# A chunked complex recurrence as scan instructions on phase-turned inputs

## The chip, the cores and the metric

One core of one Trainium2 chip runs the kernel. The metric is the device time of one execution in microseconds, as the median of several runs. Engines are named as in the profile: PE (TensorE matmul), PEld (its weight load), DVE (VectorE), ACT (ScalarE), POOL (GpSimd), SP (SyncE, which issues most DMAs).

## The reference, cut to what matters

One decoder layer for 2048 prompt positions and 8 x 4 sample positions, `D_MODEL` 1024. The part that is touched is the S5 group: 32 channel groups of 16 channels, each driving a diagonal complex state of 64 values.

```python
dt = jnp.exp(log_dt)[:, None]
mag = jnp.exp(dt * A_re); ph = dt * A_im
ar = mag * jnp.cos(ph); ai = mag * jnp.sin(ph)
...
# s[t] = a * s[t-1] + B u[t], complex, for each group and state
acum_r, acum_i, s_r, s_i = lax.associative_scan(_complex_affine_combine, (a_r, a_i, bu_r, bu_i), axis=0)
...
y = einsum(C_re, s_r) - einsum(C_im, s_i) + D * u
```

Beside it runs a short-convolution group, `y = B * conv3(C * xin)`, whose three projections are most of the matmuls of the same stage. The final states of the prompt are outputs too. Then follow GLU, output projection, memory attention and a ConvFFN.

## The kernel before

All large products are made three times (`mm3`, L369 to L373: high x high, high x low, low x high parts of weights and activations, 416 columns each). The prompt is cut into 5 pieces of up to 52 chunks (8 positions to a chunk, 256 chunks in all). The stages follow each other: u projection and tables (to about 190 us), the **convolution stage** (about 190 to 587 us), which carries the recurrence, then memory keys and values, output projection, attention, ConvFFN.

**Order of the work.** The order is written out by hand; each engine runs its instructions in program order. In the convolution stage a loop over 2 halves x 5 pieces x 2 channel tiles calls `lin_k` with 8 steps of 9 matmuls; after each step `hook` (L1183) runs: it pumps the weight splits (`W.pump`, L94 and L98) and the activation splits (`A.pump`: L158 and L159 or L161 and L162), and takes one step of the stream `slow`, and on every second call one of `slow2`. A stage has 160 hooks. A stream is a Python generator: every `yield` gives up one step. `slow` holds `state_inputs` (L878), `scan` (L1030) and `state_outputs` (L950); `slow2` holds `load_states` (L513) and `toeplitz` (L927), which must have finished (`lags`) before `state_outputs` goes on. Between the hooks DVE also makes the convolution from PSUM (L1160, L1165, L1092, L1179).

**The recurrence.** The state tile `st` holds, on 128 partitions (2 groups x 64 states), real and imaginary parts of 16 group pairs x 264 columns: 8 sample columns, then 256 chunk inputs as 16 blocks of 16. `state_inputs` makes them with fp32 matmuls (L905, L906, a PSUM pool `aux` of two banks) that ACT copies into `st` (L908, L909). `scan` runs inside the blocks: 15 positions x 2 parts x 4 DVE instructions over all groups and blocks (L1052, L1053, L1056, L1057: 120 instructions), then the block ends one after the other on POOL (L1063 to L1068: 75 instructions). `carry` (L1071, four DVE instructions of 450 columns, L1080 to L1084) adds the carried block ends times a power table `pw`, from within `state_outputs`; `enter` copies the shifted states into `scat` (DVE and ACT L971, sample columns on POOL L972), and fp32 matmuls (L1005, L1006) make the outputs, which ACT passes through GELU (L1007). The DMA loads `load(c + 2)` (uc, gc, tcn, three buffers each) are issued by SP before the matmuls of c.

## Time and profile before

| What | Value |
|---|---|
| Median of 3 runs | 3040.74 us (3035.06 to 3041.85) |
| The profiled execution, its own time | 3032.77 us |
| Its span, first to last instruction | 3031.0 us |
| PE busy | 2894.6 us (96%) |
| DVE busy | 1466.8 us (48%) |
| ACT busy | 1118.4 us (37%) |
| POOL busy | 1143.9 us (38%) |
| Mean granted TensorE clock | 0.980 |

A busy PE is not PE at its peak: matmuls overlap, and at the lower of its two clock levels the same matmul is busy for longer. So the stage is read by the number of matmuls in a stretch and the granted clock, beside the idle time. A wait in the profile is the idle time of an engine and the instruction that ended it.

### The profile page before, as it was taken

The numbers are of one execution on the slowest core, as the hardware profiler recorded it, in microseconds if no ns is written. First come the engines' busy times: TensorE is split into PE (matmuls) and PEld (weight loads), VectorE is DVE, ScalarE is ACT, GpSimd is POOL, SyncE is SP. The second block draws the span as 40 slices with busy tenths as digits, with TensorE's granted clock in tenths as the row PEclk, the third lists the DMA queues.
The fourth block names the chain that finished last, engine by engine and source line by source line (L and its number), as shares of the span: only waits on it lengthen the run. The fifth ranks groups of instructions, "written<-read, shape, count | busy, mean of one in ns | idle before, by whom it ended". The sixth has DMA issues, their size and how long they took to land.

```text
span 3031.0 us, 42111 instructions
## 1 busy us (share of the span) xinstructions
PE 2894.6 (96%) x15728; PEld 2804.2 (93%) x15728; DVE 1466.8 (48%) x2630; ACT 1118.4 (37%) x2168; POOL 1143.9 (38%) x1360
## 2 busy tenths in 40 slices
PE   8879989989999999999999999999999999999998
PEld 7778979879999999989999999998999999989997
DVE  6742986664444344354643333436433433364443
ACT  5334224454444445342422222224223222243333
POOL 3771356453332003343533323233232232345553
PEclk9889989999999999999999999999999999999999
DMA  8563244564352123565532211124322122134331
GB/s 225 145 171 106 79 141 134 173 186 130 111 167 79 52 66 108 196 222 170 193 109 63 63 56 57 55 63 143 98 59 60 50 62 63 56 119 127 116 107 54
DMA packets 387340, 335.95 MB, mean 111 GB/s; under 512 B 81121, under 2 KB 361239, under 8 KB 387103
## 3 DMA queue, kind: packets, MB, share of 16 engines
q1 hardware_dynamic: 364079, 299.30, 33.3%
q10 hardware_dynamic: 23056, 33.96, 3.1%
q8 instruction: 124, 2.03, 0.3%
q14 instruction: 81, 0.66, 0.1%
HBM read 259.98 MB, written 75.29 MB: 111 GB/s over the span
## 4 chain that ended last, share of the span: by engine, by line
PE 57%; DVE 2%; DMA 1%; POOL 1%; issue 1%; ACT 1%; SPq 0%; ACTq 0%; DVEq 0%; POOLq 0%
PE g L371 5%; PE g L372 5%; PE g L373 5%; PE u L372 5%; PE u L371 5%; PE u L373 5%; PE d L371 5%; PE d L372 5%; PE d L373 5%; PE mm L371 3%; PE mm L372 3%; PE mm L373 3%; DMA out_dram<-orow 1%; PE aux L372 1%; DMA araw<-h 0%
## 5 line engine op out<-in xcount | busy, mean ns | idle before, releaser
L98 POOL TENSOR_TENSOR wlo<-wraw,whi 128x512 fp32r<-128x512 f32 x489 | 647.7, 1348 | 895.8 <-ACT whi L94 845.6
L371 PE MATMUL mm<-xh,whi 128*128 128x416 f32 x1600 | 587.4, 367 | 15.7 <-DVE y L1179 7.3
L373 PE MATMUL mm<-xh,wlo 128*128 128x416 f32 x1600 | 571.7, 357 | 6.9 <-POOL wlo L98 6.9
L372 PE MATMUL mm<-xl,whi 128*128 128x416 f32 x1600 | 571.4, 357 | 4.7 <-POOL xl L159 4.7
L1926 DVE TENSOR_TENSOR xac<-d,xac 128x416 f32<-128x416 f32 x440 | 258.7, 591 | 249.4 <-PE d L373 246.4
L371 PEld LDWEIGHTS mm<-xh,whi 128*128 128x128 f32 x1600 | 310.0, 194 | 26.7 <-DVE xi L1160 6.3
L94 ACT CAST whi<-wraw 128x1024 fp32r<-128x1024 f32 x256 | 267.3, 1046 | 175.3 <-PE d L372 129.2
L371 PE MATMUL d<-acth,whi 128*128 128x416 f32 x880 | 310.9, 353 | 18.0 <-DVE xac L1926 17.0
L373 PEld LDWEIGHTS mm<-xh,wlo 128*128 128x128 f32 x1600 | 309.1, 193 | 11.6 <-POOL wlo L98 9.0
L372 PEld LDWEIGHTS mm<-xl,whi 128*128 128x128 f32 x1600 | 309.7, 194 | 9.0 <-POOL xl L159 6.5
L372 PE MATMUL u<-xl,whi 128*128 128x416 f32 x880 | 310.6, 353 | 1.4 <-POOL xl L159 0.7
L371 PE MATMUL g<-xh,whi 128*128 128x416 f32 x880 | 311.3, 354 | 0.0
L372 PE MATMUL g<-xl,whi 128*128 128x416 f32 x880 | 310.8, 353 | 0.0
L371 PE MATMUL u<-xh,whi 128*128 128x416 f32 x880 | 310.4, 353 | 0.3 <-ACT xh L158 0.2
L372 PE MATMUL d<-actl,whi 128*128 128x416 f32 x880 | 309.1, 351 | 0.2 <-DVE actl L1907 0.2
L373 PE MATMUL d<-acth,wlo 128*128 128x416 f32 x880 | 308.2, 350 | 0.0
L373 PE MATMUL g<-xh,wlo 128*128 128x416 f32 x880 | 306.3, 348 | 0.0
L373 PE MATMUL u<-xh,wlo 128*128 128x416 f32 x880 | 305.9, 348 | 0.0
L1092 DVE SCALAR_TENSOR_TENSOR t<-E,par,t 128x416 f32<-128x416 f32 (+1 forms) x220 | 153.9, 700 | 265.5 <-ACT t L1894 262.8
L159 POOL TENSOR_TENSOR xl<-araw,xh 128x416 fp32r<-128x416 f32 x100 | 116.0, 1164 | 380.1 <-ACT xh L158 354.2
L371 PEld LDWEIGHTS d<-acth,whi 128*128 128x128 f32 x880 | 166.2, 189 | 26.1 <-DVE xac L1926 23.8
L1903 DVE TENSOR_TENSOR t<-t,g 128x416 f32<-128x416 f32 x110 | 64.6, 587 | 258.1 <-PE g L373 257.9
(423 smaller groups left out, 4963.4 us busy)
## 6 DMA issues: line engine op xcount, KB each, us to landing
wraw<-in_w_up_dram SPq DMA_DIRECT2D x66, 512.0 KB
wraw<-in_w_gate_dram SPq DMA_DIRECT2D x66, 512.0 KB
wraw<-in_w_down_dram SPq DMA_DIRECT2D x66, 512.0 KB
araw<-x SPq DMA_DIRECT2D x120, 208.0 KB
xres<-x SPq DMA_DIRECT2D x80, 208.0 KB
x<-xo ACTq DMA_DIRECT2D x80, 208.0 KB
x<-xT ACTq DMA_DIRECT2D x40, 208.0 KB
araw<-oo SPq DMA_DIRECT2D x40, 208.0 KB
```

What stands on the lines that cost most here:

```text
L94: self.nc.scalar.copy(out=hi, in_=r)
L98: eng.tensor_tensor(out=lo[:, s], in0=r[:, s], in1=hi[:, s], op=ALU.subtract)
L159: (eng or nc.vector).tensor_tensor(out=lo[:, 0:n], in0=src, in1=hi[:, 0:n], op=ALU.subtract)
L371: PE.matmul(ps, lhsT=wh, rhs=xh, start=start, stop=False)
L372: PE.matmul(ps, lhsT=wh, rhs=xl, start=False, stop=False)
L373: PE.matmul(ps, lhsT=wl, rhs=xh, start=False, stop=stop)
L1092: V.scalar_tensor_tensor(out=out[:, 0:n], in0=E[:, tap * w:tap * w + n], scalar=c, in1=out[:, 0:n], op0=ALU.mult, op1=ALU.add)
L1903: V.tensor_tensor(out=t, in0=t, in1=ps_[:, 0:NP], op=ALU.mult)
L1926: V.tensor_tensor(out=x, in0=ps[:, 0:NP], in1=x, op=ALU.add)
```

## The change

`scan` no longer steps through the positions. The input of position j in a block is multiplied by the unit phase exp(-i j theta) of its state (`turn`), after which the recurrence has a real factor, and one `tensor_tensor_scan` over the 256 columns runs each part (`scan_blocks`); its multiplier table `dz` holds the magnitude, with zeros where a block starts. The 16 block ends are carried in the same way, two scans over all groups. `back` adds the carries times the powers of the magnitude `rp` and makes the two products of the turn back; `enter` combines them into `scat`. `turn` and `scan_blocks` are issued from the loop of `state_inputs`, one and two group pairs behind the matmuls; one `turn` in three is on POOL. The tables `ph`, `ek`, `rp` come from `phases`, stepped by `state_inputs`; `pw` and its 24 POOL products in `tables` are gone. uc, gc and tcn have two buffers, and `load(c + 2)` comes after the matmuls of c. `state_ffn_conv` is loaded one stage later, and four tiles move to a pool that opens after the convolution stage. The diff, cut to its core:

```diff
-    stf = cp.tile([128, 352], F32, name="stf")
     stc = cp.tile([128, 64], F32, name="stc")
...
-    qs = cp.tile([128, 8, 32], F32, name="qs")
-    fbp = cp.tile([128, 2, NF], F32, name="fbp")
...
+    def load_state(pl, dst, src, parts):
+        for o, n in parts:
+            r = pl.tile([128, 128], F32, tag="sr", name="sr", bufs=2)
+            SY.dma_start(out=r[0:n, :], in_=src.rearrange("b s (f p) -> (b s f) p", p=128)[o:o + n, :])
...
-    pw = cp.tile([128, 2, 16, 16], F32, name="pw")
     a4 = cp.tile([128, 2, 16], F32, name="a4")
+    qc = cp.tile([128, 2, 16], F32, name="qc")
+    mg = cp.tile([128, 16], F32, name="mg")
...
+        G.tensor_copy(out=mg, in_=mag)
+        G.tensor_scalar(out=qc[:, 0], in0=cm, scalar1=1.0, scalar2=None, op0=ALU.add)
+        G.tensor_copy(out=qc[:, 1], in_=sn)
...
-        G.tensor_copy(out=pw[:, :, :, 0], in_=pa[:, :, 8, :])
-        for m in (1, 2, 4, 8):
-            sh = [128, 16, m]
-            cmul(pre, pw[:, 0, :, m:2 * m], pw[:, 1, :, m:2 * m], pw[:, 0, :, 0:m], pw[:, 1, :, 0:m],
-                 pw[:, 0, :, m - 1:m].to_broadcast(sh), pw[:, 1, :, m - 1:m].to_broadcast(sh), sh, f"cw{m}", G)
-            yield PAUSE
...
-        uc = py.tile([128, 2, NCH], F32, tag="uc", name="uc", bufs=3)
...
+    ph = sp_.tile([128, 2, 16, 16], F32, name="ph")
+    ek = sp_.tile([128, 2, 16, 16], F32, name="ek")
...
+    def phases():
+
+        def square(q):
+            d = sp_.tile([128, 2, 16], F32, tag="sqr", name="sqr", bufs=4)
+            cmul(sp_, d[:, 0], d[:, 1], q[:, 0], q[:, 1], q[:, 0], q[:, 1], [128, 16], "csq")
+            return d
...
+        q = qc
+        for _ in range(3):
+            q = square(q)
+        unit(q)
+        yield PAUSE
...
+        V.tensor_copy(out=ph[:, :, :, 1], in_=q)
+        for m in (2, 4, 8):
+            q = square(q)
+            double(ph, m, q)
+            yield PAUSE
+        q = square(q)
+        unit(q)
+        yield "tables"
+        for m in (1, 2, 4, 8):
+            V.tensor_tensor(out=rp[:, :, m:2 * m], in0=rp[:, :, 0:m], in1=rp[:, :, m - 1:m].to_broadcast([128, 16, m]), op=ALU.mult)
...
+        for m in (2, 4, 8):
+            q = square(q)
+            double(ek, m, q)
+            yield PAUSE
...
+    def product_tile(t):
+        return sp_.tile(SQ, F32, tag="m" + t, name="m" + t, bufs=1 if t == "c" else 2)
+
+    def blocks(c):
+        return st[:, :, c, 8:264].rearrange("p r (k j) -> p r k j", j=16)
+
+    def turn(c, eng):
+
+        x, m2 = blocks(c), product_tile("b")
+        eng.tensor_tensor(out=m2, in0=x[:, ::-1], in1=ph[:, 1, c].unsqueeze(1).unsqueeze(1).to_broadcast(SQ), op=ALU.mult)
+        eng.tensor_tensor(out=x, in0=x, in1=ph[:, 0, c].unsqueeze(1).unsqueeze(1).to_broadcast(SQ), op=ALU.mult)
+        for r, op in ((0, ALU.add), (1, ALU.subtract)):
+            eng.tensor_tensor(out=x[:, r], in0=x[:, r], in1=m2[:, r], op=op)
+
+    def scan_blocks(c):
+
+        S.copy(out=dz[:, :, 1:16], in_=rp[:, c, 0:1].unsqueeze(1).to_broadcast([128, 16, 15]))
+        for r in range(2):
+            x = st[:, r, c, 8:264]
+            V.tensor_tensor_scan(out=x, data0=dz.rearrange("p k j -> p (k j)"), data1=x, initial=0.0, op0=ALU.mult, op1=ALU.add)
...
+            gc = py.tile([128, 2, 2, 128], F32, tag="tcn", name="gc", bufs=2)[:, :, 0, :]
...
+        tb = phases()
         load(0)
         usv = us_d.rearrange("(g p) j b -> j p g b", p=16)
         for j in range(NT):
             SY.dma_start(out=us_[16 * j:16 * j + 16, 1], in_=usv[j])
         load(1)
-        for _ in range(5):
-            yield PAUSE
+        for step in tb:
+            if step == "tables":
+                break
+            yield step
         V.tensor_copy(out=us_[64:128, 0], in_=us_[0:64, 1])
-        for _ in range(6):
+        for _ in range(4):
             yield PAUSE
         for c in range(16):
...
-            if c + 2 < 16:
-                load(c + 2)
...
-            yield PAUSE
+            if c + 2 < 16:
+                load(c + 2)
+            if c > 0:
+                turn(c - 1, G if c % 3 == 1 else V)
+            if c > 1:
+                scan_blocks(c - 2)
+            yield PAUSE
+            next(tb, None)
             if c % 4 == 3:
                 yield PAUSE
+        turn(15, V)
+        scan_blocks(14)
...
+        yield PAUSE
+        scan_blocks(15)
+        for _ in tb:
+            yield PAUSE
+        for _ in range(6):
...
-            tc_ = py.tile([128, 2, 2, 128], F32, tag="tcn", name="tcn", bufs=3)
...
+        def back(c):
+
+            x, m2, t = blocks(c), product_tile("b"), product_tile("c")
+            V.tensor_tensor(out=t, in0=ek[:, :, c].unsqueeze(3).to_broadcast(SQ),
+                            in1=rp[:, c].unsqueeze(1).unsqueeze(1).to_broadcast(SQ), op=ALU.mult)
+            V.tensor_tensor(out=x, in0=x, in1=t, op=ALU.add)
+            V.tensor_tensor(out=m2, in0=x[:, ::-1], in1=ph[:, 1, c].unsqueeze(1).unsqueeze(1).to_broadcast(SQ), op=ALU.mult)
+            G.tensor_tensor(out=x, in0=x, in1=ph[:, 0, c].unsqueeze(1).unsqueeze(1).to_broadcast(SQ), op=ALU.mult)
+            parts[c] = [m.rearrange("p r k j -> p r (k j)") for m in (x, m2)]
...
-            sc = py.tile([128, 2, 264], F32, tag="scat", name="scat", bufs=2)
+            sc = py.tile([128, 2, 256], F32, tag="scat", name="scat", bufs=2)
             V.memset(sc[:, :, 0:1], 0.0)
+            m1, m2 = parts.pop(c)
             for a in range(2):
                 h = slice(a * 64, (a + 1) * 64)
                 for r in range(2):
-                    o = sc[r * 64:(r + 1) * 64, a]
-                    (S.copy if r else V.tensor_copy)(out=o[:, 1:256], in_=st[h, r, c, 8:263])
-                    G.tensor_copy(out=o[:, 256:264], in_=s0[h, r, :, c])
+                    (G if r else V).tensor_tensor(out=sc[r * 64:(r + 1) * 64, a, 1:256], in0=m1[h, r, 0:255],
+                                                  in1=m2[h, r, 0:255], op=ALU.add if r else ALU.subtract)
+            for r in range(2):
+                G.tensor_tensor(out=sfin[:, r, c:c + 1], in0=m1[:, r, 255:256], in1=m2[:, r, 255:256],
+                                op=ALU.add if r else ALU.subtract)
...
-        for r in range(2):
-            carry(0, r)
-            yield PAUSE
-        for _ in range(6):
-            yield PAUSE
+        back(0)
+        yield PAUSE
+        yield PAUSE
         enter(0)
+        back(1)
         for _ in range(3):
             yield PAUSE
         for c in range(16):
-            if c + 2 < 16:
-                load(c + 2)
-            if c < 14:
-                carry(c // 2 * 2 + 2, c % 2)
             if c + 1 < 16:
                 enter(c + 1)
+            if c + 2 < 16:
+                back(c + 2)
             yield PAUSE
             uc, tcn, oc = ld.pop(c)
             sc = ent_.pop(c)
...
-                    PE.matmul(ps[:, o], lhsT=oc[:, i, :], rhs=sc[:, i, o], start=False, stop=True)
+                    PE.matmul(ps[:, o], lhsT=oc[:, i, :], rhs=sc[:, i, :] if o.start == 0 else s0s[:, 2 * c + i, :],
+                              start=False, stop=True)
                 S.activation(out=yg[:, i, :], in_=ps[:, 0:264], func=AF.Gelu_apprx_tanh)
+            if c + 2 < 16:
+                load(c + 2)
...
-            for r in range(2):
-                t = sp_.tile([128, 16, 16], F32, tag="sc", name="sc", bufs=2)
-                V.tensor_tensor(out=t, in0=x[:, r, :, :, j - 1], in1=ab[:, r], op=ALU.mult)
-                V.tensor_tensor(out=x[:, r, :, :, j], in0=x[:, r, :, :, j], in1=t, op=ALU.add)
-                yield
-                t = sp_.tile([128, 16, 16], F32, tag="sc", name="sc", bufs=2)
-                V.tensor_tensor(out=t, in0=x[:, 1 - r, :, :, j - 1], in1=ib[:, r], op=ALU.mult)
-                V.tensor_tensor(out=x[:, r, :, :, j], in0=x[:, r, :, :, j], in1=t, op=ALU.add)
-                yield
-
...
-            prev, cur = x[:, :, :, k - 1, 15], x[:, :, :, k, 15]
-            t = sp_.tile([128, 2, 16], F32, tag="cc", name="cc", bufs=2)
-            G.tensor_tensor(out=t, in0=prev, in1=pw[:, 0:1, :, 15].to_broadcast([128, 2, 16]), op=ALU.mult)
-            u = sp_.tile([128, 2, 16], F32, tag="cc", name="cc", bufs=2)
-            G.tensor_tensor(out=u, in0=prev[:, ::-1], in1=pw[:, 1:2, :, 15].to_broadcast([128, 2, 16]), op=ALU.mult)
-            G.tensor_tensor(out=cur, in0=cur, in1=t, op=ALU.add)
-            G.tensor_tensor(out=cur[:, 0], in0=cur[:, 0], in1=u[:, 0], op=ALU.subtract)
-            G.tensor_tensor(out=cur[:, 1], in0=cur[:, 1], in1=u[:, 1], op=ALU.add)
-            yield PAUSE
...
-    def carry(g0, r):
-
-        gs = slice(g0, g0 + 2)
-        sh = [128, 2, 15, 15]
-        x = st[:, :, :, 8:264].rearrange("p r g (k j) -> p r g k j", j=16)
-        c = [x[:, i, gs, 0:15, 15:16].to_broadcast(sh) for i in range(2)]
-        pb = [pw[:, i, gs, 0:15].unsqueeze(2).to_broadcast(sh) for i in range(2)]
-        d = x[:, r, gs, 1:16, 0:15]
-        t = sp_.tile(sh, F32, tag="sc", name="sc", bufs=2)
-        V.tensor_tensor(out=t, in0=c[r], in1=pb[0], op=ALU.mult)
-        V.tensor_tensor(out=d, in0=d, in1=t, op=ALU.add)
-        t = sp_.tile(sh, F32, tag="sc", name="sc", bufs=2)
-        V.tensor_tensor(out=t, in0=c[1 - r], in1=pb[1], op=ALU.mult)
-        V.tensor_tensor(out=d, in0=d, in1=t, op=ALU.add if r else ALU.subtract)
...
+        last = st[:, :, :, 8:264].rearrange("p r g (k j) -> p r g k j", j=16)[:, :, :, :, 15]
+        m2, e = product_tile("b"), product_tile("b")
+        V.tensor_copy(out=dz[:, :, 1:16], in_=rp[:, :, 15:16].to_broadcast([128, 16, 15]))
+        V.tensor_tensor(out=e, in0=last, in1=ek[:, 0:1].to_broadcast(SQ), op=ALU.mult)
+        V.tensor_tensor(out=m2, in0=last[:, ::-1], in1=ek[:, 1:2].to_broadcast(SQ), op=ALU.mult)
+        V.tensor_tensor(out=e[:, 0], in0=e[:, 0], in1=m2[:, 0], op=ALU.add)
+        V.tensor_tensor(out=e[:, 1], in0=e[:, 1], in1=m2[:, 1], op=ALU.subtract)
+        yield
+        ev = e.rearrange("p r g k -> p r (g k)")
+        for r in range(2):
+            V.tensor_tensor_scan(out=ev[:, r], data0=dz.rearrange("p g k -> p (g k)"), data1=ev[:, r],
+                                 initial=0.0, op0=ALU.mult, op1=ALU.add)
...
+        V.tensor_tensor(out=m1[:, :, :, ks], in0=e[:, :, :, 0:15], in1=ek[:, 0:1, :, ks].to_broadcast(SC), op=ALU.mult)
+        V.tensor_tensor(out=m2[:, :, :, ks], in0=e[:, ::-1, :, 0:15], in1=ek[:, 1:2, :, ks].to_broadcast(SC), op=ALU.mult)
+        for r, op in ((0, ALU.subtract), (1, ALU.add)):
+            V.tensor_tensor(out=ek[:, r, :, ks], in0=m1[:, r, :, ks], in1=m2[:, r, :, ks], op=op)
+        V.memset(ek[:, :, :, 0:1], 0.0)
+        yield
...
-    slow2.add(load_states())
+    slow2.add(load_state(py, stc, I["state_conv"][0], [(0, 64)]))
     slow2.add(toeplitz())
```

## Rows read from the trace of the kernel before

**Rows 1.** Page, part 1: busy time, share of the span, instructions.
```profile
PE 2894.6 (96%) x15728; PEld 2804.2 (93%) x15728; DVE 1466.8 (48%) x2630; ACT 1118.4 (37%) x2168; POOL 1143.9 (38%) x1360
```

**Rows 2.** Stretches: us, busy (count) PE, PEld, DVE, ACT, POOL, PEclk, DMA share, GB/s.
```profile
216.00:281.00 65.00, 54.18 (x278) 50.47 (x279) 12.83 (x22) 34.43 (x83) 12.51 (x12) 0.91 0.49 147
305.00:445.00 140.00, 123.24 (x589) 115.91 (x588) 130.04 (x191) 36.17 (x65) 56.51 (x56) 0.90 0.39 113
445.00:487.00 42.00, 42.00 (x224) 41.55 (x224) 23.99 (x35) 15.94 (x30) 36.12 (x87) 1.00 0.38 114
487.00:587.00 100.00, 91.66 (x497) 85.99 (x495) 72.92 (x147) 40.59 (x95) 49.94 (x103) 0.95 0.52 157
```

**Rows 3.** The same stretches, only instructions on the PSUM tile mm (no POOL column).
```profile
305.00:445.00 140.00, 123.11 (x587) 115.64 (x586) 13.38 (x25) 0.00 (x0) 0.90 0.39 113
445.00:487.00 42.00, 42.00 (x224) 41.51 (x223) 4.93 (x9) 0.00 (x0) 1.00 0.38 114
487.00:587.00 100.00, 49.66 (x236) 44.28 (x234) 8.38 (x16) 0.00 (x0) 0.95 0.52 157
```

**Rows 4.** Waits of PE from 195 to 500 us: total us, times, longest.
```profile
PE aux L905 <- DMA gc<-g_d: 8.8, 3, 4.6
...
PE mm L371 <- DVE y L1179: 7.3, 5, 2.1
PE mm L371 <- DVE xi L1160: 5.2, 2, 3.3
PE mm L373 <- POOL wlo L98: 4.0, 2, 2.2
...
PE aux L1006 <- DVE scat L971: 4.6, 1, 4.6
```

**Rows 5.** Tile st: duration ns min/median/max, first and last start, forms.
```profile
L971 DVE COPY scat<-st x32: 277/289/1242, 491.0 to 583.5; 64x255 f32<-64x255 f32 x32
L1052 DVE TENSOR_TENSOR sc<-st,ar x30: 578/606/1575, 305.1 to 441.7; 128x256 f32<-128x256 f32 x30
...
L1083 DVE TENSOR_TENSOR sc<-st,pw x16: 621/624/1698, 475.5 to 573.3; 128x450 f32<-128x450 f32 x16
```

**Rows 6.** Timeline of DVE (two rows) and POOL (one): start us, us, instruction.
```profile
310.56 0.60 DVE L1056 TENSOR_TENSOR sc<-st,ai 128x256 f32<-128x256 f32 x1
311.19 1.35 DVE L1057 TENSOR_TENSOR st<-st,sc 128x256 f32<-128x256 f32 x1
...
310.54 1.51 POOL L159 TENSOR_TENSOR xl<-araw,xh 128x416 fp32r<-128x416 f32 x1 [3.16 <-ACT xh L158]
```

**Rows 7.** Groups by line, 300 to 450 us: busy us, mean ns | idle before.
```profile
L1052 DVE TENSOR_TENSOR sc<-st,ar 128x256 f32<-128x256 f32 x30 | 28.3, 943 | 0.0
...
L1053 DVE TENSOR_TENSOR st<-st,sc 128x256 f32<-128x256 f32 x30 | 23.9, 796 | 1.0
```

**Rows 8.** Lines of like shape elsewhere: ns min/median/max, first and last start, forms.
```profile
L565 DVE TENSOR_TENSOR pk<-pk,cpk x4: 691/1432/1432, 96.4 to 163.4; 128x512 f32<-128x512 f32 x4
L565 DVE TENSOR_TENSOR bb<-bb,cbb x1: 424/424/424, 87.4 to 87.4; 128x256 f32<-128x256 f32 x1
...
L1032 DVE TENSOR_SCALAR ai<-pw x1: 163/163/163, 296.6 to 296.6; 128x16 f32<-128x16 f32 x1
...
L584 POOL TENSOR_TENSOR ogt<-ctn,pat x12: 1049/1056/1495, 109.0 to 172.1; 128x512 f32<-128x512 f32 x12
...
L1666 POOL TENSOR_TENSOR skl<-ckv,skh x32: 723/864/1811, 1315.4 to 1384.7; 128x256 fp32r<-128x256 f32 x32
```

**Rows 9.** Timeline of PE, two successive half pairs of the output matmuls.
```profile
578.54 0.68 PE L1005 MATMUL aux<-uc,tcn 128*128 128x256 f32 x2
...
579.85 0.68 PE L1005 MATMUL aux<-uc,tcn 128*128 128x256 f32 x2
```

**Rows 10.** Groups of POOL by line, 487 to 587 us.
```profile
L972 POOL COPY scat<-s 64x8 f32<-64x8 f32 x64 | 25.8, 403 | 2.5
```

**Rows 11.** Waits of the SP queue, 195 to 610 us.
```profile
SPq L875 <- PE aux L906: 6.9, 6, 3.0
```

More of the change, by code (lines that the diff above doesn't have):

```diff
@@ L276, in tile_hymba_step @@
     V.memset(halc, 0.0)
-    stf = cp.tile([128, 352], F32, name="stf")
     stc = cp.tile([128, 64], F32, name="stc")
-    qs = cp.tile([128, 8, 32], F32, name="qs")
-    fbp = cp.tile([128, 2, NF], F32, name="fbp")
-    fbs = cp.tile([128, 8, 2, NF], F32, name="fbs")
     cbp = cp.tile([128, 2, 4], F32, name="cbp")
@@ L511, in load_params @@
         yield PAUSE
-    def load_states():
-        fl = I["state_ffn_conv"][0].rearrange("b s (f p) -> (b s f) p", p=128)
-        cl = I["state_conv"][0].rearrange("b s (f p) -> (b s f) p", p=128)
-        for dst, src, o, n in ((stf, fl, 0, 128), (stf, fl, 128, 128), (stf, fl, 256, 96), (stc, cl, 0, 64)):
-            r = py.tile([128, 128], F32, tag="sr", name="sr", bufs=2)
-            SY.dma_start(out=r[0:n, :], in_=src[o:o + n, :])
+    def load_state(pl, dst, src, parts):
+        for o, n in parts:
+            r = pl.tile([128, 128], F32, tag="sr", name="sr", bufs=2)
+            SY.dma_start(out=r[0:n, :], in_=src.rearrange("b s (f p) -> (b s f) p", p=128)[o:o + n, :])
             for _ in range(6 if o else 8):
@@ L870, in load_u @@
     def load_u(c):
-        uc = py.tile([128, 2, NCH], F32, tag="uc", name="uc", bufs=3)
+        uc = py.tile([128, 2, NCH], F32, tag="uc", name="uc", bufs=2)
         for i in range(2):
@@ L883, in load @@
             uc = load_u(c)
-            gc = py.tile([128, 2, 2, 128], F32, tag="tcn", name="gc", bufs=3)[:, :, 0, :]
+            gc = py.tile([128, 2, 2, 128], F32, tag="tcn", name="gc", bufs=2)[:, :, 0, :]
             SY.dma_start(out=gc, in_=g_d[:, g2, :])
@@ L917, in state_inputs @@
             rs_.append(r)
-        for _ in range(7):
+        yield PAUSE
[3 more added lines that the diff above has]
+        for _ in range(6):
             yield PAUSE
@@ L923, in state_inputs @@
             V.tensor_copy(out=s0[:, i].rearrange("p b g -> p (b g)"), in_=ps[:, 0:128])
+            sv = s0s.rearrange("p (g a) b -> p a b g", a=2)
+            for a in range(2):
+                G.tensor_copy(out=sv[i * 64:(i + 1) * 64, a], in_=s0[a * 64:(a + 1) * 64, i])
     lags = [0]
@@ L958, in load @@
             uc = load_u(c)
-            tc_ = py.tile([128, 2, 2, 128], F32, tag="tcn", name="tcn", bufs=3)
+            tc_ = py.tile([128, 2, 2, 128], F32, tag="tcn", name="tcn", bufs=2)
             SY.dma_start(out=tc_, in_=to_d[:, g2])
             ld[c] = (uc, tc_[:, :, 0, :], tc_[:, :, 1, :])
+        parts = {}
+        def back(c):
[6 more added lines that the diff above has]
+            parts[c] = [m.rearrange("p r k j -> p r (k j)") for m in (x, m2)]
         def enter(c):
-            sc = py.tile([128, 2, 264], F32, tag="scat", name="scat", bufs=2)
+            sc = py.tile([128, 2, 256], F32, tag="scat", name="scat", bufs=2)
             V.memset(sc[:, :, 0:1], 0.0)
+            m1, m2 = parts.pop(c)
             for a in range(2):
@@ L1013, in state_outputs @@
             store(out=ysd[j], in_=ysm[j * 16:(j + 1) * 16])
-        state_out(sp_, st[:, :, :, 263], 16, [o[0, 0].rearrange("(g a) n -> g (a n)", a=2) for o in (sre_p, sim_p)])
+        state_out(sp_, sfin, 16, [o[0, 0].rearrange("(g a) n -> g (a n)", a=2) for o in (sre_p, sim_p)])
         yield PAUSE
-    ar2 = sp_.tile([128, 2, 16], F32, name="ar2")
-    ai2 = sp_.tile([128, 2, 16], F32, name="ai2")
     def state_out(pl, src, n, dsts):
@@ L1060, in scan @@
-        for k in range(1, 16):
-            prev, cur = x[:, :, :, k - 1, 15], x[:, :, :, k, 15]
-            t = sp_.tile([128, 2, 16], F32, tag="cc", name="cc", bufs=2)
-            G.tensor_tensor(out=t, in0=prev, in1=pw[:, 0:1, :, 15].to_broadcast([128, 2, 16]), op=ALU.mult)
-            u = sp_.tile([128, 2, 16], F32, tag="cc", name="cc", bufs=2)
-            G.tensor_tensor(out=u, in0=prev[:, ::-1], in1=pw[:, 1:2, :, 15].to_broadcast([128, 2, 16]), op=ALU.mult)
-            G.tensor_tensor(out=cur, in0=cur, in1=t, op=ALU.add)
-            G.tensor_tensor(out=cur[:, 0], in0=cur[:, 0], in1=u[:, 0], op=ALU.subtract)
-            G.tensor_tensor(out=cur[:, 1], in0=cur[:, 1], in1=u[:, 1], op=ALU.add)
-            yield PAUSE
@@ L1212, in tile_hymba_step @@
     srs.close()
+    lp = ctx.enter_context(pool("late", side="left"))
+    stf = lp.tile([128, 352], F32, name="stf")
+    qs = lp.tile([128, 8, 32], F32, name="qs")
+    fbp = lp.tile([128, 2, NF], F32, name="fbp")
+    fbs = lp.tile([128, 8, 2, NF], F32, name="fbs")
     skv = ExitStack()
@@ L1467, in tile_hymba_step @@
     slow.add(conv_states())
+    slow.add(load_state(p3, stf, I["state_ffn_conv"][0], [(0, 128), (128, 128), (256, 96)]))
     p3_load(ORDER3[0])
```

36 lines of the change are left out of this document (28 added, 8 removed).

## The prediction

> **What bounds the kernel now.** I read the page's busy table first: PE is busy for 96% of the span [rows 1], so only time in which PE waits, or runs at its lower clock, can be won. Then the stretches of the convolution stage, cut where the work of its side stream changes [rows 2], and the same cut for the products on the PSUM tile mm [rows 3]. From 445 to 487 us PE does 224 products in 42.0 us at granted clock 1.00: 0.1875 us each, the rate of a fed PE. From 305 to 445 us, where `scan` runs, it does 587; at 0.1875 us these are 110 us, but the stretch lasts 140. So **30 us are lost there**: 140 - 123 = 17 us PE is idle, the rest goes to a mean clock of 0.90, which falls after such gaps (0.90 is part of the time at 2.4 GHz and part at 1.2). In the same stretch DVE is busy 130 of 140 us, and the waits of PE name DVE: y for 7.3 us, xi for 5.2 us [rows 4]. DVE is the bound of that stretch, through the convolution's evictions that stand in its queue behind the scan.
>
> Why is DVE so full? The scan's instructions have a median of 0.606 us [rows 5], but their means are 0.80 to 0.94 us; the four lines (first and last shown, 30 times each) come to 101 us [rows 7], where 120 x 0.61 = 73 would be undisturbed. The other 28 us are blocking by POOL: a POOL subtraction starts at 310.54, the DVE instruction of 310.56 takes 0.60 us, and the next takes 1.35 while POOL finishes [rows 6]. POOL was busy 56.5 us [rows 2], so each us of POOL's busy time costs a saturated DVE about 0.5 us. I use that half below.
>
> The outputs stretch, 487 to 587 us, does 236 products (44 us) and 16 group pairs of fp32 matmuls. Two halves of a pair start 1.31 us apart [rows 9], so a pair is 2.6 us and the 16 are 42 us: 86 us of work and some transposes in 100 us, so about 12 us are lost, 4.6 of them a first wait on scat [rows 4]. The inputs stretch, 216 to 281 us, is 65 us long with DVE busy for only 12.8 us and POOL for 12.5 [rows 2].
>
> **The change, part by part.** *The order of the steps.* A stage has 160 hooks. Before, the stream asks for 38 + 79 + 48 = 165 steps. After, 4 + 4 + 20 + 1 + 6 = 35 for the inputs, 7 for `scan`, 42 for the outputs: 84. With `load_states` cut to one part `toeplitz` is done after 9 + 22 = 31 second hooks, near hook 62, and the outputs run from there to about hook 105, all under products; some 70 hooks carry nothing.
>
> *Removed: the scan's 120 DVE and 75 POOL instructions.* The stretch of 30 us lost becomes plain products: **-30 us**. The small POOL table `pw` in the u stage goes too; PE's waits there are for other work, so I cost it at nothing (0 to -2).
>
> *Added in the inputs loop.* Per `turn` two instructions of 512 columns (0.691 [rows 8]) and two of 256 (0.424 [rows 8]): 2.23 us; ten fall on DVE in the loop, 22.3 us. No row shows a scan instruction. Its nearest rows are two-input DVE instructions of the same 256 columns: 0.424 below [rows 8], the slowest, 1.575, above [rows 5]; I take the median of the strided form, 0.606, since a dependent chain should not beat a plain stream. 28 of them fall in the loop: 17.0 us (11.9 to 44.1). `phases` issues some 76 small DVE instructions before the loop, where DVE waits for data anyway, and 43 within it, between 0.163 us [rows 8] and 0.29; at 0.2 that is 8.6 us. With the 12.8 us of now DVE needs 61 us. POOL gets five turns of 2 x 1.05 + 2 x 0.72 = 3.5 us [rows 8], 17.7 us, and is busy 30 us; half of it blocks DVE, 15 us. DVE then needs 76 us for a stretch of 65: **+11 us**.
> Three new waits are in there. ACT fills the single `dz` and so waits for the scans before; behind it in ACT's queue stand the copies of `st` that free the two aux banks, and PE waits for those, so DVE may fall only about three pairs (12 us) behind before PE stops. A DVE scan after a POOL turn waits for POOL, and the evictions behind it wait too. And with two buffers each load stands at the head of SP's queue until PE has done that pair, with the activation and weight loads behind it; PE waited 8.8 us for gc [rows 4] and SP 6.9 us for PE [rows 11] with three buffers. I take 0.25 us a pair, **+4 us** (0 to +12).
>
> *The outputs.* Before, a pair cost DVE four instructions of 0.624 and two copies of 0.289 [rows 5], 3.1 us; after, three of 512 columns in `back` (2.07) and two of 256 in `enter` (0.85): 2.9 us. POOL loses its 64 sample copies, 25.8 us [rows 10], and gets one of 512 columns (1.05), two of 256 (1.44), two small ones and the copy of today (0.25 each, an estimate below the 0.403 us of the copies that it loses [rows 10]): 3.25 us a pair. With the 0.2 us of other work per us of time that the inputs stretch shows [rows 2], over the 6 us of a pair (2 hooks x 9 x 0.1875 + 2.6), DVE needs 4.1 us and POOL 4.4. DVE blocked for half of POOL's time: 6.3 us, against 6.0 of PE. So this stretch is just DVE-bound, 16 x 0.3 = 5 us; the weight splits of the second half (12 on POOL, which cost PE 4.0 us of waits before [rows 4]) now fall into it, another 5. About 11 us lost in place of 12: **-1 us** (-8 to +36).
>
> *After the stage* the GLU finds its y long stored, which spares it a half-clock start: **-2 us** (0 to -4). The later load of the ffn state is three transposes and copies under products; the moved tiles cost nothing.
>
> Sum: -30 + 11 + 4 - 1 - 2 = -18 us. Against the profiled execution's 3032.8 us that is 3015; the median of the runs lies 8 us above that execution, so I predict **3023 us**.
>
> **A rule that speaks against the change.** The rows show DVE standing still behind a POOL instruction [rows 6]. The Trainium skill, SBUF — State Buffer, section "Who interferes with whom", says that a DVE instruction with two SBUF inputs and a POOL instruction that reads SBUF hold a shared port pair exclusively, the later one blocked whole. By that rule POOL's full time would count, which is the second rival below. The Trainium skill, DVE: opcode table, instruction layouts, handler registers and perf-mode slots, section "Datapath and trigger behaviour", says that the built-in tensor_tensor_scan runs at half throughput. As an estimate a 256-column scan would then cost like a 512-column instruction, 0.691 us, and the sum would be 2.4 us worse; nothing below uses it.
>
> **The rivals.** *1. Neither loop binds.* DVE catches up in the free hooks and the ring of three pairs takes the lag: then -30, the outputs at PE's own rate (-5), -2 and loads 0 to +4 give 3005 us or a little less. For it: 52 idle us of DVE in the inputs stretch. Against: the lag of 11 us comes within one stretch.
> *2. Slower: DVE and POOL exclude each other whole.* Then the inputs need 61 + 30 = 91 us (+26), the outputs 16 x 8.5 = 136 us (+36): -30 - 2 + 26 + 36 + 4 = +34, 3075 us. It turns from gain to loss where about 0.65 of POOL's busy time blocks DVE instead of 0.5. For it: the 1.35 us in [rows 6]. Against: the scan stretch of today shows half, and DVE's PSUM instructions need no turn.
> *3. The scan is slow,* near 1.575 us: 28 x 0.97 = +27 us in the inputs loop, 3050 us; it decides from about 1.2 us a scan. Against it: nothing in the trace; for it only that each column depends on the one before.
> *4. It cancels:* the block share lies near 0.65, or SP's blocked loads cost 12 us with a pair or two of waits more; 3036 to 3046 us.
>
> **How the numbers follow.** The forecast with its terms, 3006 to 3034 us, gets 0.48; rival 1 0.14, rival 2 0.15, rival 3 0.08, rival 4 0.15. A measurement of this kernel tells about 0.2%, 6 us, from no change. Faster: 0.48 + 0.14 = 0.62; same: 0.15; slower: 0.23. The likeliest case's own range is 3006 to 3034. The range for 8 in 10 takes in rival 4, rival 3 and most of rival 1, and ends below rival 2: 3002 to 3056 us.
>
> **What would show it.** Right: the products between the inputs and the outputs at 0.19 us each with clock 1.00, about 30 us less between the first and last product of the stage before the loops' costs; DVE over 85% busy in the inputs loop and scans near 0.6 us median; outputs at 6 to 6.5 us a pair. Wrong: outputs at 8 us a pair with both DVE and POOL near full (rival 2); scan medians above 1 us (rival 3); PE waits on gc, uc or tcn over 10 us (the loads); a stage that still ends near 587 us.

## The result, and the profile after

| | Before | After |
|---|---|---|
| Median of the runs made together | 3041.30 us (3035.06 to 3045.68, 4 runs) | 3058.13 us (3054.09 to 3059.26, 4 runs) |
| Ratio after / before | | 1.0055, interval 1.0034 to 1.0075 |
| Span of the profiled execution | 3031.0 us | 3052.0 us |

The kernel became **slower by 17 us**; the forecast was 18 us faster, and 3058 lies 2 us above the range. The page of after, part 1, answers [rows 1]:

```profile
PE 2904.3 (95%) x15728; PEld 2804.3 (92%) x15728; DVE 1474.1 (48%) x2698; ACT 1109.6 (36%) x2152; POOL 1166.6 (38%) x1304
```

PE does the same 15728 instructions, and no engine's share moves by more than a point: the cost has to be looked for by stretches. Those of after, with the columns of [rows 2]: the whole inputs loop, one piece of the free hooks, and the outputs loop in three pieces.

```profile
196.00:312.00 116.00, 83.77 (x384) 76.72 (x383) 105.12 (x229) 49.52 (x116) 49.16 (x46) 0.82 0.42 118
...
390.00:420.00 30.00, 25.75 (x116) 23.43 (x115) 24.82 (x33) 9.19 (x19) 25.57 (x33) 0.78 0.55 171
420.00:450.00 30.00, 26.98 (x135) 25.04 (x135) 22.67 (x31) 5.67 (x14) 23.71 (x32) 0.90 0.49 154
450.00:480.00 30.00, 28.56 (x151) 27.18 (x152) 24.98 (x36) 8.60 (x19) 23.79 (x32) 0.93 0.56 174
```

DVE, 12.8 us busy of 65 in the inputs before [rows 2], is now busy for 105 of 116, and PE's clock there is 0.82. In the outputs DVE and POOL are both busy for about 80%. Between the two loops, the same view for the products on mm alone:

```profile
320.00:366.00 46.00, 46.00 (x246) 45.51 (x245) 7.05 (x12) 0.00 (x0) 1.00 0.58 155
```

246 products in 46.0 us, 0.187 us each: a fed PE, where the scan held it before.

**The balance by stretches.** A hook follows each 9 products of the stage, so the start of the stage's product 9k dates hook k. Read from the traces (us from the start of the span, as in the views; "160" is the first such product of the next stage):

| hook | before | after | e5 no work | e6 no loads | e7 no tables | e4 spread | e12 spread, pad |
|---|---|---|---|---|---|---|---|
| 8 | 201.5 | 197.8 | 203.9 | 202.5 | 199.3 | 203.0 | 201.4 |
| 32 | 283.8 | 306.8 | 300.6 | 305.2 | 298.3 | 287.6 | 286.3 |
| 40 | 297.7 | 320.8 | 314.7 | 323.7 | 312.4 | 308.7 | 308.0 |
| 72 | 352.6 | 375.2 | 369.1 | 379.0 | 366.8 | 370.3 | 369.2 |
| 112 | 449.7 | 512.5 | 486.4 | 511.6 | 505.5 | 466.6 | 465.4 |
| 160 | 658.0 | 665.8 | 641.7 | 665.8 | 660.0 | 639.5 | 638.4 |
| span | 3031.0 | 3052.0 | 3022.8 | 3051.1 | 3043.6 | 3026.9 | 3012.6 |

After less before: -3.7 up to hook 8 (the stage's first product starts between 182.4 and 188.4 us in the profiles of all the kernels here, so this is scatter); from hook 8 to 40, the inputs, 123.0 - 96.1 = **+26.9**; from 40 to 160, which holds the scan and the outputs of before and the outputs of after, 345.0 - 360.4 = **-15.4**; from 160 to the end 2386.2 - 2373.0 = **+13.2**. The sum is +21.0, the difference of the spans. The forecast had +15, -33 and 0.

The last term is not in the recurrence at all. 9.0 us of it lie in the ConvFFN; the other 4 lie between hook 160 and the ConvFFN, a piece that scatters by 6.6 us over the profiles of all the kernels here. Tile d, the third product of each triple (ns min/median/max, first and last start), of before, after, e1 and e12, in this order:

```profile
L373 PE MATMUL d<-acth,wlo x880: 345/349/354, 1516.9 to 3012.8; 128*128 128x416 f32 x176
```
```profile
L369 PE MATMUL d<-acth,wlo x880: 345/353/356, 1528.9 to 3033.8; 128*128 128x416 f32 x176
```
```profile
L369 PE MATMUL d<-acth,wlo x880: 345/353/548, 1524.2 to 3025.5; 128*128 128x416 f32 x176
```
```profile
L369 PE MATMUL d<-acth,wlo x880: 345/349/354, 1497.8 to 2994.2; 128*128 128x416 f32 x176
```

From the first of these rows' start times to the last, the stage lasts 1495.9 us before and 1504.9 after, with the same instructions. The median goes from 349 to 353 ns where tiles were moved (after, e1) and back to 349 where a pad moves the stage's tiles back (e12). All profiles divide so: before and the four runs with the pad (e8, e9, e11, e12) have 349 ns and 1495.9 to 1499.0 us, the nine with moved tiles and no pad 353 ns and 1501.3 to 1505.4 us.

### The profile page after: what moved, and what is told of

Its sections match the earlier page's. It is cut to its first block, busy times and chain, and to the rows that moved or that the text cites. A ratio compares the mean times of both kernels' runs of the same rounds, so it can differ in the third digit from the quotient of the medians.

```text
span 3052.0 us, 42118 instructions
## 1 busy us (share of the span) xinstructions
PE 2904.3 (95%) x15728; PEld 2804.3 (92%) x15728; DVE 1474.1 (48%) x2698; ACT 1109.6 (36%) x2152; POOL 1166.6 (38%) x1304
## 4 chain that ended last, share of the span: by engine, by line
PE 57%; DVE 3%; DMA 1%; issue 1%; POOL 1%; ACT 1%; SPq 0%; ACTq 0%; DVEq 0%; POOLq 0%
PE g L368 5%; PE g L369 5%; PE g L367 5%; PE u L368 5%; PE u L367 5%; PE u L369 5%; PE d L367 5%; PE d L369 5%; PE d L368 5%; PE mm L368 3%; PE mm L369 3%; PE mm L367 3%; PE aux L368 1%; DVE t L1173 1%; POOL wlo L98 0%
## 5 line engine op out<-in xcount | busy, mean ns | idle before, releaser
L98 POOL TENSOR_TENSOR wlo<-wraw,whi 128x512 fp32r<-128x512 f32 x489 | 644.0, 1340 | 896.8 <-ACT whi L94 839.0
L94 ACT CAST whi<-wraw 128x1024 fp32r<-128x1024 f32 x256 | 267.0, 1046 | 172.5 <-PE d L368 129.5
L367 PEld LDWEIGHTS mm<-xh,whi 128*128 128x128 f32 x1600 | 308.2, 193 | 12.8 <-ACT whi L94 4.0
```

What stands on the lines that cost most here:

```text
L94: self.nc.scalar.copy(out=hi, in_=r)
L98: eng.tensor_tensor(out=lo[:, s], in0=r[:, s], in1=hi[:, s], op=ALU.subtract)
L367: PE.matmul(ps, lhsT=wh, rhs=xh, start=start, stop=False)
```

## The experiments

Theories: **A**, the moved tiles cost the ConvFFN its 9 us. **1**, both loops are bound by the instructions of DVE and POOL. **2**, the two-buffer loads bind them. **3**, the tables in front of `us` hold back the inputs. Ratios are to the kernel before on the same chip; after stands at 1.0055.

**e1, the tiles of after in the kernel before.**

```diff
-    stf = cp.tile([128, 352], F32, name="stf")
...
-    qs = cp.tile([128, 8, 32], F32, name="qs")
...
-    pw = cp.tile([128, 2, 16, 16], F32, name="pw")
+    pw = rsp.tile([128, 2, 16, 16], F32, name="pw")
...
+    lp = ctx.enter_context(pool("late", side="left"))
+    stf = lp.tile([128, 352], F32, name="stf")
+    qs = lp.tile([128, 8, 32], F32, name="qs")
```

> The kernel before, with its tiles in SBUF where the changed kernel has them: the four tiles in the late pool, the power table in the pool that closes after the convolution stage, 48 spare columns in the constant pool, the ffn state loaded one stage later. No instruction of the recurrence differs. Theory A (the place of the tiles in SBUF sets the spacing of the products in the ConvFFN): the ConvFFN, 9 us longer in the changed kernel, is 9 us longer here too, and the kernel is 5 to 10 us slower than the kernel before. Rival (the 9 us belong to that one execution or chip): no difference beyond 3 us, spacing as before.

Measured: 3042.96 us, ratio 1.0026 (1.0015 to 1.0037), hook 160 at 659.0 us (before: 658.0), from there to the end 11.7 us more than before, ConvFFN 1501.3 us. Without any part of the new recurrence about 8 us of the loss are there: theory A.

**e2, POOL out of both loops.** `enter` and the products for `sfin` are moved to DVE like the two shown.

```diff
-                turn(c - 1, G if c % 3 == 1 else V)
+                turn(c - 1, V)
...
-            G.tensor_tensor(out=x, in0=x, in1=ph[:, 0, c].unsqueeze(1).unsqueeze(1).to_broadcast(SQ), op=ALU.mult)
+            V.tensor_tensor(out=x, in0=x, in1=ph[:, 0, c].unsqueeze(1).unsqueeze(1).to_broadcast(SQ), op=ALU.mult)
```

> The changed kernel with every instruction that turn, back and enter give POOL issued on DVE. Theory B (DVE and POOL block each other in the two loops, so the sum of both is what counts): outputs from 8.2 us a pair to 6.0 to 6.8, inputs no slower than now, in all 15 to 30 us faster than the changed kernel. Rival (DVE alone has too much work): both loops slower, 8 to 9 us a pair in the outputs, 10 us or more slower than the changed kernel.

Measured: 3050.14 us, ratio 1.0041 (1.0025 to 1.0056). The outputs of e2, columns of [rows 2]:

```profile
390.00:420.00 30.00, 22.69 (x117) 20.65 (x116) 28.43 (x54) 9.47 (x19) 11.69 (x14) 0.89 0.53 171
420.00:450.00 30.00, 24.67 (x132) 22.61 (x130) 28.10 (x52) 5.55 (x15) 11.17 (x13) 0.97 0.50 166
450.00:480.00 30.00, 29.04 (x153) 26.97 (x152) 28.09 (x55) 9.00 (x20) 8.51 (x12) 0.92 0.55 170
```

With POOL's share moved over, DVE is busy for 94%, waits no more for POOL, and the outputs are no faster: from hook 72 to 112 136.3 us, in after 137.3. Neither number that was expected came: the kernel gains 0.14%, inside the intervals. What is saved in blocking and waiting is spent on the instructions taken over. So not the sharing between the engines alone binds, but the amount of work per pair.

**e3, the copy of `us` on POOL.**

```diff
-        V.tensor_copy(out=us_[64:128, 0], in_=us_[0:64, 1])
+        G.tensor_copy(out=us_[64:128, 0], in_=us_[0:64, 1])
```

> The changed kernel with the one copy of the sample inputs (the wait of 13.1 us of PE at the start of the inputs loop) moved from DVE, where it stands behind 76 small table instructions, to POOL. Theory C (the start is bound by the rate of DVE, which has the tables to finish before the first turn): PE starts earlier and waits later, 0 to 6 us faster. Rival (the place of that copy in DVE's queue is the cost): 13 us and the clock after it come back, about 20 us faster.

Measured: 3057.75 us, ratio 1.0071 (1.005 to 1.0091). PE's waits from 195 to 320 us:

```profile
PE aux L979 <- DMA gc<-g_d: 11.1, 5, 4.3
PE aux L980 <- POOL us L972: 8.3, 1, 8.3
```

The same waits in after:

```profile
PE aux L980 <- DVE us L972: 13.1, 1, 13.1
PE aux L979 <- DMA gc<-g_d: 11.6, 5, 4.3
```

The wait for us, 13.1 us behind DVE, shrinks to 8.3, and hooks 8 to 32 take 108.7 us instead of 109.0: to bring the first product forward gains nothing while DVE's queue stays as long.

**e4, more hooks for each pair.**

```diff
             next(tb, None)
+            yield PAUSE
...
                 back(c + 2)
             yield PAUSE
+            yield PAUSE
+            yield PAUSE
```

> The changed kernel with one more step of the stream per pair in the inputs loop and two more in the outputs loop, so that both loops use hooks that are idle now (58 + 74 of 160 steps). Theory B (both loops ask for more DVE and POOL time than a pair's products last): PE is fed in both loops, 25 to 45 us faster than the changed kernel and 10 to 25 faster than the kernel before; the wait at the start of the inputs stays. Rival (the loops are bound by chains of waits inside a pair, not by the amount of work): less than 10 us faster.

Measured: **3026.54 us, ratio 0.9963** (0.9952 to 0.9975), against 1.0055 of after. The outputs of e4:

```profile
425.00:465.00 40.00, 40.00 (x224) 39.03 (x223) 35.93 (x49) 11.97 (x27) 30.16 (x39) 1.00 0.54 168
465.00:505.00 40.00, 40.00 (x224) 39.04 (x223) 34.14 (x49) 14.29 (x29) 28.86 (x38) 1.00 0.52 162
```

PE is busy without a gap at clock 1.00, while DVE is at 85 to 90%: the same instructions, with 9.35 us of time to a pair (hooks 88 to 96, two pairs, take 18.7), leave PE no gap. More time to a pair hides waits between the engines as well as work, so this run doesn't tell the two apart.

**e5, the loops without their DVE and POOL work.**

```diff
-            if c > 0:
-                turn(c - 1, G if c % 3 == 1 else V)
-            if c > 1:
-                scan_blocks(c - 2)
...
-                back(c + 2)
...
-                    (G if r else V).tensor_tensor(out=sc[r * 64:(r + 1) * 64, a, 1:256], in0=m1[h, r, 0:255],
-                                                  in1=m2[h, r, 0:255], op=ALU.add if r else ALU.subtract)
+                    (S.copy if r else V.tensor_copy)(out=sc[r * 64:(r + 1) * 64, a, 1:256], in_=st[h, r, c, 8:263])
```

> The changed kernel with its loads of two buffers, its tables and its steps, but without the DVE and POOL work of the recurrence in the two loops: turns and in-block scans are left out of the inputs loop, back is left out of the outputs loop and enter is the plain copy of before (DVE and ACT); so the states and what follows from them are not the reference's. Theory 1 (both loops are bound by the instructions of DVE and POOL): the outputs fall from 8.2 to about 6.2 us a pair (-32 us), the inputs, from hook 8 to hook 32, from 109 to about 95 us (the tables stay): some 3012 us. Theory 2 (the loads with two buffers bind both loops): the outputs stay at about 8 us a pair and the inputs at over 103 us, 3045 to 3058 us.

Measured: 3020.96 us, ratio 0.9945 (0.9925 to 0.9965). Outputs of e5:

```profile
433.00:457.00 24.00, 24.00 (x138) 23.15 (x137) 8.12 (x21) 11.71 (x27) 6.63 (x18) 1.00 0.61 195
```

Hooks 88 to 96, four pairs, take 23.9 us, 6.0 a pair (the pairs of the kernel before follow each other at 6.2), with two buffers and the loads behind the matmuls. From hook 72 to 112 it is 117.3 us instead of 137.3, from 8 to 32 96.7 instead of 109.0. Theory 1: 20 us of the outputs, where 32 were expected, and 12 of the inputs are the instructions.

**e6, no loads after the second pair.** The outputs loop has the same edit with its own tiles.

```diff
             if c + 2 < 16:
-                load(c + 2)
+                ld[c + 2] = (uc, gc)
```

> The changed kernel with only the first two pairs of each loop loaded: the later pairs take the tiles of the first two again, so that no load waits for a buffer (its results are those of the wrong inputs). Theory 1 (instructions of DVE and POOL): within 6 us of the changed kernel's 3058, the outputs at 8 us a pair. Theory 2 (the loads): the outputs at 6.2 us a pair, 3020 to 3030 us. Between them, a share of the inputs: gc is waited for 8.4 us in the changed kernel, which would go: 3050 us.

Measured: 3053.71 us, ratio 1.0053 (1.0035 to 1.0072): 1.0055 within its interval. Outputs from hook 72 to 112: 132.6 us; DVE's waits in them (390 to 500 us):

```profile
DVE scat L1073 <- POOL st L1062: 17.6, 11, 3.0
```

In after the same row says 16.5 us. In the inputs hook 32 comes 6.3 us sooner after hook 8, of which 1.8 are left at hook 40. PE's waits for gc there, 11.6 us in after, are gone, but another has grown, from 1.3 us in after:

```profile
PE aux L979 <- ACT st L983: 9.5, 3, 4.5
```

Theory 2 falls; the loads are worth 2 to 6 us.

**e7, no tables.** `rp` and `ek` are set like `ph`, and the steps stay.

```diff
+        V.memset(ph, 0.5)
...
-        for m in (2, 4, 8):
-            q = square(q)
-            double(ph, m, q)
-            yield PAUSE
```

> The changed kernel with the tables of phases set to a constant instead of being computed (some 76 small DVE instructions ahead of the inputs loop and 43 in it are left out, and the states are wrong). Theory 3 (the tables hold back the inputs' first product): the wait for us of 13 us goes, and the hooks 8 to 32 take 92 to 97 us instead of 109: 3040 to 3046 us. Rival (the turns and scans bind the inputs whatever the start): the first product comes 13 us sooner, but hook 32 is reached within 5 us of the changed kernel: 3053 to 3058 us.

Measured: 3049.13 us, ratio 1.0034 (1.0021 to 1.0047). Hooks 8 to 32 take 99.0 us instead of 109.0. The tables, those ahead of the loop and those in it, cost 10 us there, a little less than theory 3 had. In the whole time the difference to after is 0.21%, within what the two intervals allow, and 3049 lies between the two ranges that were expected. PE's waits from 195 to 320 us:

```profile
PE aux L960 <- DMA gc<-g_d: 10.6, 5, 4.4
...
PE aux L961 <- DVE us L953: 0.9, 1, 0.9
```

The wait for us is gone (13.1 us in after); the one for gc stays as it was (11.6).

**e8 and e12, e4 with a pad.** e12 is e8 again, on the chip of e11.

```diff
+    lpad = lp.tile([128, 464], F32, name="lpad")
+    V.memset(lpad[:, 0:1], 0.0)
     skv = ExitStack()
```

> The spread version (one more step a pair in the inputs loop, two more in the outputs loop) with a pad of 464 floats a partition in the pool that opens after the convolution stage, so that the tiles of the ConvFFN stand at the addresses of the kernel before. Theory (the moved tiles cost the ConvFFN 5 to 9 us): 3026 - 5 = 3021 us, and the stage from its first to its last product d takes 1496 us as before. Rival (the 9 us come from the moved activation tiles, which the pad doesn't move back, or from elsewhere): 3026 us and 1505 us.

> e8 unchanged, on the chip of e11, to compare the two: 0.994 of the kernel before, as in its first run; if its gain was one of that chip, nearer to e4's 0.9963.

Measured: 3020.08 us, **ratio 0.9941** (0.9923 to 0.9959), and 3016.88 us, **0.9949** (0.9935 to 0.9962); e4 had 0.9963. The ConvFFN takes 1499.0 us in e8 and 1496.4 in e12 (1505.4 in e4); e12's row is shown above. In the whole time the gain over e4, 4 to 7 us, is no wider than the intervals; the stage's own time shows it. This is the best version: some 19 us below before on the same chips, where after stands 17 above.

**e9, e8 with the tables behind `us` and beside the first pairs.** The scans follow one pair behind the turns, so the loop runs to c = 19.

```diff
-        for step in tb:
-            if step == "tables":
-                break
-            yield step
+        for _ in range(8):
+            yield PAUSE
         V.tensor_copy(out=us_[64:128, 0], in_=us_[0:64, 1])
...
-                turn(c - 1, G if c % 3 == 1 else V)
+                turn(c - 5, G if c % 3 == 2 else V)
```

> e8 with the copy of us ahead of the tables, the tables stepped by the first pairs of the inputs loop instead of before it, and turns and scans five and six pairs behind the matmuls instead of one and two. Theory 3 (the tables in front of us hold back the inputs by about 10 us, as e7 showed with the tables left out): hooks 8 to 32 go in about 75 us instead of 84.5, the wait for us falls from 13 us to under 4, and the time is some 3010 us, 8 to 10 us under e8. Rival (the DVE work that is late now is late later: PE waits for st or for the convolution's tiles in the middle of the loop instead): within 3 us of e8, 3017 to 3023 us.

Measured: 3030.81 us, ratio 0.9981 (0.997 to 0.9993), **slower than e8**. From hook 8 to 56 it takes 129.5 us against 139.8 of e8; then comes, as the only long wait of PE from 320 to 380 us,

```profile
PE aux L1129 <- DVE sf L1139: 12.7, 1, 12.7
```

The 10 us are won and more than paid back: the turns that were put off stand in DVE's queue ahead of the sample states. From 345 to 380 us the clock is at 0.80, and, counted from hook 8, e9 is 5 us behind e8 at hook 72 and 8 at hook 160.

**e10, only the outputs spread.**

```diff
                 back(c + 2)
             yield PAUSE
+            yield PAUSE
+            yield PAUSE
```

> The changed kernel with two more steps a pair in the outputs loop alone; the inputs loop is that of the changed kernel. Theory 1 (the outputs loop asks DVE and POOL for 8 us a pair, and its 20 us of loss go where a pair has more products beside it): the outputs' products run at 0.19 us each at clock 1.00 as in e4, and the time is 3058 - 25 = 3033 us. Rival (the gain of e4 was made in the inputs loop, whose later end pushed the outputs): over 3045 us.

Measured: 3035.63 us, ratio 1.0002 (0.9992 to 1.0012): theory 1, with 16 of the 25 us. Of the 0.92% between after and e4, 0.53% (16 us) come from the outputs and the other 0.39% (12 us) from the inputs. The clock wasn't full throughout:

```profile
400.00:425.00 25.00, 23.72 (x129) 22.40 (x127) 20.70 (x26) 6.25 (x12) 22.89 (x28) 1.00 0.58 187
425.00:450.00 25.00, 22.68 (x108) 21.49 (x107) 23.06 (x32) 10.08 (x22) 18.73 (x23) 0.86 0.53 165
```

**e11, e9 with more steps behind the inputs.** They are eight, not the nine of the expectation: the last turn, at c = 19, had its step in e9 already.

```diff
-            if c % 4 == 3:
+            if c % 4 == 3 or c > 15:
                 yield PAUSE
...
-        for _ in range(6):
+        for _ in range(11):
             yield PAUSE
```

> e9 with one step more for each of the last four turns and five more behind the last scan, nine in all, so that DVE has worked off the late turns before PE transposes sf. Theory (e9 gained its 10 us at the start and gave 12.7 of them back in the one wait for sf behind DVE's backlog): the wait for sf falls under 2 us, 10 to 13 us less than e9, 3010 to 3020 us, and 3 to 8 us less than e8 on the same chip. Rival (what is late in DVE only meets the next wait, in the outputs): within 4 us of e9.

Measured: 3024.94 us, ratio 0.997 (0.996 to 0.998); e12 on the same chip 0.9949. PE's waits from 320 to 560 us:

```profile
PE aux L1110 <- POOL scat L1073: 8.8, 1, 8.8
PE aux L1129 <- DVE sf L1139: 5.7, 1, 5.7
```

The wait is halved and a new one stands behind it: mostly the rival. What DVE owes is due at the first place where PE needs a state.

## Why the prediction was wrong, step by step

Between the forecast, -18 us, and the profiles, +21, lie 39 us: 11.9 in the inputs, 17.6 from hook 40 to 160, 13.2 behind it, less the 3.7 of scatter ahead. The steps behind them:

**The scan's 30 us: right.** PE runs fed between the loops, and waits for nothing from 310 to 370 us. From hook 40 to 72 a hook costs 1.70 us after; before, hooks 40 to 112 (298 to 450 us, with the scan beside them) cost 2.11, which over these 72 is 30 us.

**The prices of the new instructions: right, and the contention on top of them nearly so.** Tile st of after (ns min/median/max, first and last start):

```profile
L949 DVE TENSOR_TENSOR_SCAN st<-dz,st x32: 657/680/1776, 231.7 to 308.3; 128x256 f32<-128x256 f32 x32
...
L942 DVE TENSOR_TENSOR st<-st,mb x22: 410/424/1523, 231.0 to 305.7; 128x256 f32<-128x256 f32 x22
L1061 DVE TENSOR_TENSOR mb<-st,ph x16: 691/697/1667, 368.5 to 486.5; 128x512 f32<-128x512 f32 x16
L1062 POOL TENSOR_TENSOR st<-st,ph x16: 1258/1267/1641, 369.3 to 487.3; 128x512 f32<-128x512 f32 x16
```

0.424 and 0.691 were the forecast's own; the scan was taken at 0.606 and has 0.680. The Trainium skill, DVE: opcode table, instruction layouts, handler registers and perf-mode slots, section "Datapath and trigger behaviour", says that this scan runs at half throughput; the trace agrees, 0.680 us for 256 columns beside 0.691 for a plain instruction of 512. Rival 3 (scans near 1.575 us) didn't happen.

**"`phases` issues some 76 small DVE instructions before the loop, where DVE waits for data anyway": wrong, up to 10 us.** DVE groups by line, 196 to 312 us:

```profile
L949 DVE TENSOR_TENSOR_SCAN st<-dz,st 128x256 f32<-128x256 f32 x32 | 26.6, 871 | 1.5 <-ACT dz L946 1.5
L942 DVE TENSOR_TENSOR st<-st,mb 128x256 f32<-128x256 f32 x22 | 12.7, 616 | 0.4
L939 DVE TENSOR_TENSOR mb<-st,ph 128x512 f32<-128x512 f32 x11 | 9.3, 848 | 0.0
L940 DVE TENSOR_TENSOR st<-st,ph 128x512 f32<-128x512 f32 x11 | 8.4, 766 | 0.4
...
L554 DVE TENSOR_TENSOR csq<-sqr 128x16 f32<-128x16 f32 x9 | 4.7, 520 | 0.1
```

Scans take 26.6 us and turns 30.4. The 119 instructions of the tables (many lines like the last) keep DVE busy for 18.8 us up to 216 us and for 13.6 behind it, where the sum had 8.6 inside the loop and nothing ahead of it. Behind 216 us DVE is busy for 86 us in all; some 6 of them are the turn and the four scans that the sum left behind the loop, and the other 80 compare with its 76. DVE's idle time ahead of the loop was no cover: the tables ended at 216 us, and the loop then needed DVE from its first pair on. e7 puts the tables, both parts together, at 10 us; no run takes out one part alone. If the parts add up, the inputs' 26.9 us at hook 40 are e5's 12.3, e7's 9.9 and e6's 1.8 (forecast for the loads: 4), and 3 us stay open. The prediction named waits for gc of over 10 us as a sign that the loads cost more than forecast; they came, 11.6 us, and e6 puts the loads at 2 to 6 us all the same.

**"So this stretch is just DVE-bound", 6.3 us a pair: wrong, 17 us.** From hook 72 to 112 there are 67.5 us of products (40 x 9 x 0.1875) and 42 of pairs [rows 9]; the 137.3 us hold 27.8 of loss in place of 11, and e5 holds 7.8 of unknown cause. Groups of DVE and POOL, 390 to 480 us of after:

```profile
L1073 DVE TENSOR_TENSOR scat<-st,mb 64x255 f32<-64x255 f32 x24 | 23.2, 967 | 15.2 <-POOL st L1062 14.9
L1058 DVE TENSOR_TENSOR mc<-ek,rp 128x512 f32<-128x512 f32 x12 | 13.9, 1162 | 0.4
L1060 DVE TENSOR_TENSOR st<-st,mc 128x512 f32<-128x512 f32 x11 | 12.1, 1098 | 0.4
L1061 DVE TENSOR_TENSOR mb<-st,ph 128x512 f32<-128x512 f32 x11 | 9.4, 857 | 0.4
```
```profile
L1073 POOL TENSOR_TENSOR scat<-st,mb 64x255 f32<-64x255 f32 x24 | 22.6, 942 | 1.8
L1062 POOL TENSOR_TENSOR st<-st,ph 128x512 f32<-128x512 f32 x12 | 16.7, 1388 | 6.4 <-DVE mb L1061 5.1 <-DVE scat L1068 1.3
L98 POOL TENSOR_TENSOR wlo<-wraw,whi 128x512 fp32r<-128x512 f32 x8 | 11.2, 1415 | 0.0
L159 POOL TENSOR_TENSOR xl<-araw,xh 128x416 fp32r<-128x416 f32 x7 | 8.5, 1220 | 0.0
L1076 POOL TENSOR_TENSOR sfin<-st,mb 128x1 f32<-128x1 f32 x24 | 7.7, 343 | 0.9
```

Twelve pairs in 90 us are 7.5 us each. Over the undisturbed 0.424 and 0.691, the new DVE instructions lost 25.0 us (13.0 at L1073, 5.7 at L1058, 4.5 at L1060 and 1.8 at L1061); without that DVE needs (72.5 - 25.0) / 12 = 4.0 us a pair, as forecast (4.1).

The mis-sized term is **POOL: 73.1 / 12 = 6.1 us a pair instead of 4.4**. Its instruction in `back` took 1.39 us instead of 1.05, the two in `enter` 1.88 instead of 1.44, and its splits and products of the convolution 2.1 instead of 1.2: the share of other work was taken from the inputs stretch, and the weight splits of the second half were put in as a lump of 5 us instead of as POOL time. The sum also had no term for the **chain** between the engines: DVE stood 14.9 us for the POOL product in `back`, and POOL 6.4 for DVE.

Blocking alone, if all that loss is put down to POOL, was a third of POOL's busy time (25.0 / 73.1), blocking and waiting together 0.55. The prediction's half was read from a saturated DVE (130 of 140 us busy), and in after DVE is idle for a fifth of the time. In e2, where it is busy for 94%, the same sum over its five new lines gives 15.1 us of loss for 31.4 of POOL, 0.48; the largest, in the same window:

```profile
L1073 DVE TENSOR_TENSOR scat<-st,mb 64x255 f32<-64x255 f32 x45 | 27.4, 610 | 0.7
```

With 6.1 in place of 4.4 the prediction's half would have given 4.0 + 3.05 = 7.1 us a pair.

That is the direction of rival 2, but not its mechanism: whole exclusion would have made all of POOL's time count, a third did, and e2, which takes POOL's share of the two loops out, is no faster in the outputs. By the rule of the Trainium skill, SBUF — State Buffer, section "Who interferes with whom", the shared ports are held exclusively. The trace agrees for a single collision (below). That POOL's whole time would count in a loop, which the prediction drew from it, the trace doesn't show: 25.0 of 73.1 us.

**"Some 70 hooks carry nothing": seen, and not used.** Time per pair was the lever: e4 spends 48 of these hooks and turns +0.55% into -0.37%, with every instruction kept.

**"The moved tiles cost nothing": wrong**, 9.0 us of the ConvFFN in the profiles; e1 has 5.4 of it without the change, and the pad takes it back but for 0.5 to 3.1. **The -2 us after the stage** can't be told apart in any run: e1's span from hook 160 on is 2384.6 us and after's 2386.2.

## What to carry to other kernels

A faster instruction sequence gains only if each loop that it moves to has the time for it: sum the work of each engine per pass of that loop, what already runs there included, and compare it with what PE needs for a pass, before looking at idle time elsewhere. Where an idle stretch follows, give the passes more of it rather than moving work between engines, and don't put work off that a later wait must have. A change of SBUF layout is part of a change's time and can be tried by itself.
